# Two more pairs of gate blocks in seven-product form, and the retention norm moved to GpSimd and ScalarE one chunk later

## The chip, the cores and the metric

The kernel runs on one core of a Trainium2 chip. The metric is device time in microseconds (us), the median of several runs; smaller is better. The engines are TensorE (PE, with its weight loads shown as PEld), VectorE (DVE), ScalarE (ACT), GpSimd (POOL) and SyncE (SP, which only issues transfers here). Each works through its own instructions in program order; they wait for one another through semaphores.

## The reference

One decoder block on 1024 tokens of width 1024, in float32: two parallel token mixers (chunkwise retention and dilated attention), gated and merged, then an MLP. What matters here is the retention branch and its gate.

```python
proj = h @ w_in
rq, rk, rv, rg = parts[0], parts[1], parts[2], parts[3]   # 4 heads: dk 256, dv 512
...
def step(state, inp):                                     # a chunk of 128 tokens, 8 chunks
    s = einsum('bhid,bhjd->bhij', qi, ki) * inner_decay
    o = einsum('bhij,bhje->bhie', s, vi) + einsum('bhid,bhde->bhie', qi, state) * q_decay
    state = state * chunk_decay + einsum('bhjd,bhje->bhde', ki * k_decay, vi)
...
ro = (ro - mu) * rsqrt(var + GN_EPS)                      # mean and variance over dv
ro = ro * gn_g + gn_b
ret_out = (silu(rg) * ro) @ w_ret_out
```

## The kernel before, in words

All products are done in float32 accuracy by three passes (`mm3`, L203): each operand is split into a high and a low part, and low x high, high x low and high x high are summed, so that a product of 128x128 weights with 512 columns takes three matmuls (L207, L209, L211). The order of the work on each engine is the order in which the program writes it (a manual schedule).

The stages around the change, in time: the values of one attention group, then the **pair stage** (`queries_keys`, L1259): the projections whose results are kept in DRAM are done as pairs of two blocks of 128 output columns by `Blocks` (L226), in a Strassen-Winograd form with seven block products (`ORDER`) where eight would be needed; a pair is 7 x 4 x 3 = 84 matmuls. `PAIRS` (L1158) lists 22 pairs by kind: r (queries and keys of retention), a and k (attention), g (gates) and s (the fourth of each head's four 128-column blocks of the retention gate rg, two heads to a pair). Then the **values stage** (`values`, L1384). In both, `mod_turn` (L1243) loads one 512 KB row block of the modulation weights at a fixed number of product steps and multiplies it on DVE.

Then the **chunk loop** (`chunk`, L715), 32 chunks: heads h = 0 to 3, c = 0 to 7, g = 8h + c. In one chunk TensorE does, in this order:

- kv: the new part of the state from k and v of this chunk, two halves of three matmuls (not in c = 7)
- `rg_mm`: steps of the projection of the other three gate blocks of each head (classical: a block has eight steps of six matmuls, two halves of 512 tokens), all but the last step of this chunk; the number of steps of each chunk stands in `RG` (L693), three nearly everywhere
- `s_kt(g + 1)` (L630): the scores sT of the next chunk and the transposed keys kT; ACT and DVE then make sm, smh, sml and kh, kl from them
- o: the output of this chunk, six matmuls with the state (not in c = 0) and three with v
- `on_T` (L670): oT, the transposes of the chunk before's normalized output `on`, copied by ACT to a tile per head
- the last `rg_mm` step of the chunk

On the other engines: DVE updates the state (L745), ACT casts it to its high part (L749) and DVE subtracts for the low part (L750). `jit_qk` makes the high and low parts j of a later chunk's queries and keys (ACT L616, POOL L617). DVE takes the statistics of o (`bn_stats`, `bn_aggr`, L772 to L774), POOL raises the variance to the power -1/2 (L775), DVE multiplies by the decay (L776) and normalizes o from PSUM to SBUF (`onm`, L778). A finished gate block gets its Silu on ACT (`rg_out`, L705). In chunks c = 0 to 3 of a later head, `u_final` (L681) scales and shifts a quarter of the last head's output on ACT (L688), multiplies it by the gate on DVE (L690) and stores it. `ahead(2)` splits the next gate weights (`split_w`, L197 on ACT and L198 on DVE).

Space in PSUM (eight banks): "mm" has two buffers of two banks (the gate blocks take one each in turn), "s" has four single banks for everything else, o among it. In SBUF the tag "E" has twelve tiles of 128x1024, for the normalized output of two heads and for the gates.

Of the kernel before, what the change touches and what calls it, by code (L numbers as in the profile page):

```python
# [11 lines left out]
F32 = mybir.dt.float32  # L12
# [9 lines left out]
H = 4  # L22
# [15 lines left out]

CS_ID = 0
CS_KDEC = 128  # L40
CS_QD = 132
CS_QD2 = 136
CS_ONE = 140
CS_MH = 141
CS_W = 149
# [95 lines left out]
def block_kernel(ctx, tc, io, stop=None, dbg=None):  # L141
# [3 lines left out]
    def fv(t):  # L145
        return t.bitcast(F32)
# [18 lines left out]

    def ps_mm(name):
        return PS["p"].tile([P, 2, 512], F32, tag="mm", bufs=2, name=name)

    def ps_s(name, shape=(P, 512)):
        return PS["p"].tile(list(shape), F32, tag="s", bufs=PS["n"], name=name)  # L170
# [339 lines left out]
        R["p"] = ret_ctx.enter_context(tc.tile_pool(name="ret", bufs=1, reuse_waits="tile"))  # L510

    def etile(name, dt=F32):
        return R["p"].tile([P, 1024], dt, tag="E", bufs=12, name=name)

# [112 lines left out]
            R[n] = p.tile([P, 2, P], F32R, tag=n, bufs=1, name=n + "00")  # L627
        R["j"] = p.tile([P, 2, 4, C], F32R, tag="j", bufs=2, name="j2")

    def s_kt(i):  # L630

        p = R["p"]
        g = i
        h, c = divmod(g, NC)
        t = hd["j", g]
        ps = ps_s(f"sT{h}{c}")
        for i in range(2):
            nc.tensor.matmul(ps[:, :2 * C], t[:, 0, 2 + i, :], t[:, :, i, :], start=i == 0, stop=False,
                             skip_group_check=True)
            nc.tensor.matmul(ps[:, :C], t[:, 1, 2 + i, :], t[:, 0, i, :], start=False, stop=i == 1,  # L640
                             skip_group_check=True)
# [10 lines left out]
        nc.scalar.copy(sm, ps[:, :C])  # L652
# [12 lines left out]
        if pk is not None:  # L665
            nc.vector.scalar_tensor_tensor(flat(kl), flat(pk), kd, fv(flat(kh)), op0=ALU.mult, op1=ALU.subtract)
            hd["k", g] = (kh, kl)
        nc.vector.tensor_sub(sml, sm, fv(smh))

    def on_T(h, c):  # L670

        po = ps_s(f"oT{h}{c}", (P, 4, P))
        on = hd["o", h, c]
        if c == 0:
            hd["on", h] = [etile(f"on{h}{e}") for e in range(4)]
        for e in range(4):
            nc.tensor.transpose(po[:, e, :], on[:, e * P:(e + 1) * P], ident)
        for e in range(4):
            nc.scalar.copy(hd["on", h][e][:, c * C:(c + 1) * C], po[:, e, :])

    def u_final(h, es=range(4), queue=nc.sync):  # L681
        for e in es:
            i = h * 4 + e
            t = hd["on", h][e]
            for hf in range(2):
                neg = 16 if hf == i % 2 else 0
                b = t[:, 512 * hf:512 * hf + 512]
                nc.scalar.activation(b, b, AF.Identity, scale=gnv[0][:, neg + i:neg + i + 1],  # L688
                                     bias=gnv[1][:, neg + i:neg + i + 1])
            nc.vector.tensor_mul(t, t, hd["srg", h, e])  # L690
            queue.dma_start(y_d[h][:, 2 * (i % 2):2 * (i % 2) + 2, e // 2], t.rearrange("p (t x) -> p t x", t=2))
# [12 lines left out]

    def rg_out(h, c):  # L705

        if "rgs" in hd:
            e = {1: 0, 2: 0, 4: 1, 5: 1, 7: 2}[c]
            hd["srg", h, e] = etile(f"srg{h}{e}")
            nc.scalar.activation(hd["srg", h, e], flat(hd.pop("rgs")), AF.Silu)  # L710
        if c == 6:
            hd["srg", h, 3] = etile(f"srg{h}3")
            nc.sync.dma_start(hd["srg", h, 3], srg_d[h])

    def chunk(h, c, ahead, w=None):  # L715
        p = R["p"]
# [17 lines left out]
                kvs.append(kv)  # L734
        if g == 0:
            s_kt(1)
        rg_mm(1 if g == 0 else RG[h][c] - 1)
        for i, kv in enumerate(kvs):
            if g == 0:
                nc.scalar.copy(sh1[:, i, :], kv)  # L740
# [3 lines left out]
            else:  # L744
                nc.vector.scalar_tensor_tensor(st[:, i, :], st[:, i, :], float(GAMMA[h] ** C), kv,  # L745
                                               op0=ALU.mult, op1=ALU.add)
        if g > 0:
            for i in range(len(kvs)):
                nc.scalar.copy(sh1[:, i, :], st[:, i, :])  # L749
                nc.vector.tensor_sub(sl1[:, i, :], st[:, i, :], fv(sh1[:, i, :]))  # L750
        if g == 0:
            jit_qk(2)
        ahead(2)
        if 0 < g < NG - 1:
            s_kt(g + 1)
        po = ps_s(f"o{h}{c}")
        if c > 0:
            t = hd["j", g]
            for i in range(2):
# [5 lines left out]
            jit_qk(g + 2)  # L765
        if g > 0:
            on_T(*divmod(g - 1, NC))
        rg_mm(0 if g == 0 else 1)
        bn = p.tile([P, 6], F32, tag="bn", bufs=2, name=f"bn{h}{c}")
        ba = p.tile([P, 2], F32, tag="ba", bufs=2, name=f"ba{h}{c}")  # L770
        gr = p.tile([P, 1], F32, tag="gr", bufs=2, name=f"gr{h}{c}")
        nc.vector.bn_stats(bn, po)  # L772
        nc.vector.bn_aggr(ba, bn)
        nc.vector.tensor_scalar(gr, ba[:, 1:2], ct[:, CS_QD2 + h:CS_QD2 + h + 1], GN_EPS, op0=ALU.mult, op1=ALU.add)  # L774
# [6 lines left out]
        if h > 0 and c < 4:  # L781
            u_final(h - 1, (c,))

    def wsplit(ap):
        return ap, split_w
# [5 lines left out]
    srg_d = [dram.tile([P, S], F32, name=f"srgd{h}") for h in range(H)]  # L791
    h12_d = [dram.tile([P, 2, 512], F32, name=f"h12d{m}") for m in range(4)]
    xn, wa = [], []

# [330 lines left out]
    def sums_of_h(name, ms=range(4)):  # L1125

        for m in ms:
# [18 lines left out]
            if name != "t4":  # L1146
# [42 lines left out]
    def a_out(q, n, x, y=None):  # L1189
# [19 lines left out]
        if n in ("12", "21"):  # L1209
# [4 lines left out]
            elif pair[0] == "k":  # L1214
                dst = ak_d[pair[2], i]
            elif pair[0] == "s":
                dst = srg_d[2 * pair[1] + i]
            else:
                return
            nc.sync.dma_start(dst, OA[q][i])  # L1220
# [210 lines left out]
    steps.add(more_values, manual=True)  # L1431
    steps.add(queries_keys, manual=True)

    for h in range(H):
        for c in range(NC):
            steps.add((lambda h, c: lambda ahead, *w: chunk(h, c, ahead, *w))(h, c),
                      ([wsplit(io["w_rg"][3 * h + (0, 2, 5).index(c)])] if c in (0, 2, 5) else []),
                      manual=True)


# [390 lines left out]
    def att_step(pair, a):  # L1831

        def body(*args):
            ps = ps_mm(f"ak{pair}1{a}")
            gen = with_sums(proj_gen(ps, args[-1]))
            if a == 1:
# [991 lines left out]
def _constants():  # L2828
# [9 lines left out]
    for h in range(H):  # L2838
# [4 lines left out]
        cst[:, CS_QD + h] = np.exp(lg * (i + 1))  # L2843
        cst[:, CS_QD2 + h] = np.exp(2 * lg * (i + 1))
    cst[:, CS_ONE] = 1.0
    cst[:, CS_MH:CS_MH + 8] = -0.5

# [16 lines left out]
def pack(x, c, w_ada, b_ada, norm1_g, w_in, rel_bias, ret_gn_g, ret_gn_b,  # L2864
# [17 lines left out]
        "w_rg": _cols(w[:, 4096:6144].reshape(1024, 4, 4, P)[:, :, :3].reshape(1024, 1536)),  # L2882
        "w_rg2": _pairs(w[:, 4096:6144].reshape(1024, 4, 4, P)[:, :, 3].reshape(1024, 512)),
# [33 lines left out]
```

## Time and profile before

| | before |
|---|---|
| median of 3 runs | 2175.04 us (2174.86 to 2175.66) |
| the profiled execution | 2173.28 us, span 2171.3 us |
| mean granted TensorE clock | 0.999 |
| busy: PE, DVE, ACT, POOL | 99%, 70%, 44%, 8% of the span |
| pair stage, first to last matmul start | 179.7 to 595.7 us |
| chunk loop | about 712 to 981 us |

In the rows below, a line of the timeline has the start in us, the duration, the engine, the line of the kernel, the operation, out<-in, the shape and how many were merged into it; in brackets stands the engine's idle time before it and what ended that. A group's row has the count, the busy time in us and the mean ns of one, and then the idle time before. A row of waits has the waiting engine and its output, what it waited for, the total in us, how often, and the longest.

### The profile page before, as it was taken

Reading aid. Unit: us, or ns where it says so; the run is one execution under the profiler, and the core shown is the slowest. Engines: PE = TensorE matmul, PEld = TensorE weight load, DVE = VectorE, ACT = ScalarE, POOL = GpSimd, SP = SyncE. Lnnn points to the kernel's source line nnn. Section 1 sums busy time; section 2 is a strip of 40 time slices with the busy share of each in tenths; the row PEclk is TensorE's granted clock in tenths of the full one; section 3 lists DMA queues with packets and bytes.
Section 4 is the critical chain, followed back from the end, with each engine's and each line's share of the span. In section 5 each row is a group of like instructions: output and inputs, shape, how many; then the busy total and the mean of one; then the engine's idle time right before and its main releaser. Section 6 shows DMA issues by size and latency. Waiting matters only on the chain. (4 is left out here: it accounts for less than half of the span.)

```text
span 2171.3 us, 27289 instructions
## 1 busy us (share of the span) xinstructions
PE 2144.7 (99%) x10036; PEld 1782.4 (82%) x10036; DVE 1520.4 (70%) x2358; ACT 959.3 (44%) x1757; POOL 165.7 (8%) x199
## 2 busy tenths in 40 slices
PE   8999999999999999999999999999999999999998
PEld 6888888888887788888888888888778888888887
DVE  6886777777656677776667644677876665877855
ACT  5543322323334455556656625434454455533413
POOL 0001111100001112211110000001000000000003
PEclk9999999999999999999999999999999999999999
DMA  9859998835588744436877366653144435645322
GB/s 383 282 208 309 285 306 265 243 117 194 186 301 303 234 148 151 160 127 197 218 194 196 115 245 211 217 191 132 64 175 160 150 136 193 253 135 173 109 88 78
DMA packets 162674, 425.18 MB, mean 196 GB/s; under 512 B 28005, under 2 KB 55916, under 8 KB 159468
## 3 DMA queue, kind: packets, MB, share of 16 engines
q1 hardware_dynamic: 150264, 374.90, 48.3%
q0 software_dynamic: 9584, 48.24, 9.9%
q8 instruction: 79, 1.29, 0.2%
q10 hardware_dynamic: 2692, 0.30, 0.1%
q14 instruction: 55, 0.45, 0.1%
HBM read 324.13 MB, written 160.32 MB: 223 GB/s over the span
## 5 line engine op out<-in xcount | busy, mean ns | idle before, releaser
L207 PE MATMUL qap<-hh,qaw 128*128 128x512 f32 x264 | 102.7, 389 | 0.0
L209 PE MATMUL qap<-hl,qaw 128*128 128x512 f32 x264 | 102.7, 389 | 0.0
L211 PE MATMUL qap<-hh,qaw 128*128 128x512 f32 x264 | 102.7, 389 | 0.0
L617 POOL TENSOR_TENSOR j<-qk,j 128x512 fp32r<-128x512 f32 x32 | 42.8, 1338 | 454.8 <-ACT j L616 454.8
L2235 POOL TENSOR_TENSOR accnf<-accnf,sqnf 128x256 f32<-128x256 f32 (+1 forms) x18 | 16.6, 922 | 609.6 <-ACT sqnf L2231 609.6
L2339 ACT ACTIVATE a<-a 128x512 f32<-128x512 f32 x48 | 30.3, 631 | 72.8 <-DVE a L2338 71.3
L749 ACT CAST stateh<-state 128x512 fp32r<-128x512 f32 x54 | 32.9, 622 | 57.8 <-DVE state L745 55.7
L209 PEld LDWEIGHTS qap<-hl,qaw 128*128 128x128 f32 x264 | 49.5, 188 | 10.4
L211 PEld LDWEIGHTS qap<-hh,qaw 128*128 128x128 f32 x264 | 49.6, 188 | 10.3
L207 PEld LDWEIGHTS qap<-hh,qaw 128*128 128x128 f32 x264 | 49.5, 188 | 10.2
L2547 ACT CAST w2h<-w2s 128x512 fp32r<-128x512 f32 x36 | 22.4, 621 | 80.3 <-DVE w2s L2585 80.3
L264 DVE TENSOR_TENSOR fw<-w1r,fw 128x512 fp32r<-128x512 f32 x48 | 32.9, 688 | 33.6 <-ACT fw L254 33.6
L264 DVE TENSOR_TENSOR qaw<-wa,qaw 128x512 fp32r<-128x512 f32 x66 | 44.0, 687 | 9.4 <-ACT qaw L254 9.4
L2070 DVE TENSOR_TENSOR rwl<-rwl,rwh 128x1024 fp32r<-128x1024 f32 x25 | 30.2, 1221 | 29.0 <-ACT rwh L2100 29.0
L207 PE MATMUL fp<-h2h,fw 128*128 128x512 f32 x128 | 50.0, 390 | 0.0
L209 PE MATMUL fp<-h2l,fw 128*128 128x512 f32 x128 | 49.8, 389 | 0.0
L211 PE MATMUL fp<-h2h,fw 128*128 128x512 f32 x128 | 49.8, 389 | 0.0
L207 PE MATMUL roa<-rh,rwl 128*128 128x512 f32 x128 | 49.8, 389 | 0.0
L209 PE MATMUL roa<-rl,rwh 128*128 128x512 f32 x128 | 49.8, 389 | 0.0
L211 PE MATMUL roa<-rh,rwh 128*128 128x512 f32 x128 | 49.8, 389 | 0.0
L1603 ACT ACTIVATE P<-P,ng 128x128 f32<-128x128 f32 (+1 forms) x96 | 41.9, 438 | 17.6 <-DVE ng L1595 17.5
L292 DVE TENSOR_TENSOR qat<-qat,qap 128x512 f32<-128x512 f32 x22 | 15.1, 688 | 42.8 <-PE qap L211 35.8
(3089 smaller groups left out, 7187.8 us busy)
## 6 DMA issues: line engine op xcount, KB each, us to landing
cossin<-in_w_ada_dram SPq DMA_DIRECT2D x32, 512.0 KB, 3.5
v<-vd SPq DMA_DIRECT2D x32, 512.0 KB, 4.3
w1r<-in_w_ff_dram SPq DMA_DIRECT2D x32, 512.0 KB, 4.6
yt<-y POOLq DMA_DIRECT2D x24, 512.0 KB, 7.5
xsd<-as SPq DMA_DIRECT2D x24, 512.0 KB, 3.1
w2r<-in_w_ff2s_dram SPq DMA_DIRECT2D x24, 512.0 KB, 6.4
em<-in_w_ada_dram SPq DMA_DIRECT2D x16, 512.0 KB, 10.2
wrvs<-in_w_rv_dram POOLq DMA_DIRECT2D x16, 512.0 KB, 9.8
```

Source lines behind the costliest of these rows:

```text
L207: nc.tensor.matmul(o, wl, xh, start=first, stop=False, skip_group_check=skip)
L209: nc.tensor.matmul(o, wh, xl, start=False, stop=False, skip_group_check=skip)
L211: nc.tensor.matmul(o, wh, xh, start=False, stop=last, skip_group_check=skip)
L264: nc.vector.tensor_sub(t[:, 512:], src, fv(t[:, :512]))
L292: nc.vector.tensor_sub(u, u, b)
L617: nc.gpsimd.tensor_sub(t[:, 1], src, fv(t[:, 0]))
L749: nc.scalar.copy(sh1[:, i, :], st[:, i, :])
L1603: nc.scalar.activation(v, v, AF.Exp, bias=ng[:, blk:blk + 1], accum_out=st[:, g, blk, 2 + a:3 + a])
L2070: nc.vector.tensor_sub(lo, fv(lo), fv(hi))
L2235: (nc.vector if f == 7 else nc.gpsimd).tensor_add(G["acc", key], G["acc", key], sq)
L2339: nc.scalar.activation(o, o, AF.Relu)
L2547: nc.scalar.copy(hi, src)
```

## The change

- The third and the fourth gate block of each head are now one s pair: four s pairs where there were two (`PAIRS` ends in "agagassss", 24 pairs), and eight blocks are left to the chunk loop where there were twelve. Two gates per head are loaded back from DRAM, in c = 4 and c = 6.
- `RG` falls to 64 steps in all. Weights are requested one chunk ahead of the chunk in which their block begins.
- A gate block takes two single banks of a new tag "rg" with two buffers, and its two Silus follow its last product at once. o gets a tag of its own, "o", with two buffers. At the first attention step PSUM is laid out anew (`banks(False)`).
- The normalization of chunk g is one ACT activation with scale and bias, issued in chunk g + 1 behind `s_kt` and ahead of o. The decay is folded into the epsilon (`CS_EQ`), so no multiplication by the decay is left; POOL makes scale and bias in three operations of 128x1.
- The two low halves of the state are apart: one inside `s_kt`, the other behind the statistics of o. `ahead(2)` moves behind the statistics. The multiplication and store of `u_final` come one chunk later.
- `on_T` copies two blocks at once into a double tile (tag "EO", four buffers); "E" has four buffers, for gates alone.
- `mod_turn` issues a load every two steps, where before it was every 16/7.

```diff
+    def ps_rg(name):
+        return PS["p"].tile([P, 512], F32, tag="rg", bufs=2, name=name)
+    def ps_o(name):
+        return PS["p"].tile([P, 512], F32, tag="o", bufs=2, name=name)
...
     def etile(name, dt=F32):
-        return R["p"].tile([P, 1024], dt, tag="E", bufs=12, name=name)
+        return R["p"].tile([P, 1024], dt, tag="E", bufs=4, name=name)
...
-    def s_kt(i):
+    def s_kt(i, mid=None):
...
             hd["k", g] = (kh, kl)
+        if mid:
+            mid()
         nc.vector.tensor_sub(sml, sm, fv(smh))
...
-        for e in range(4):
-            nc.scalar.copy(hd["on", h][e][:, c * C:(c + 1) * C], po[:, e, :])
+        for e in range(2):
+            nc.scalar.copy(hd["on2", h][e][:, :, c * C:(c + 1) * C], po[:, 2 * e:2 * e + 2, :])
...
-    RG = ((6, 2, 2, 3, 3, 3, 3, 2),) + ((3,) * NC,) * (H - 1)
+    RG = (6, 2, 2, 2, 1, 1, 2, 3), (3, 2, 2, 2, 1, 1, 2, 3), (3, 2, 2, 2, 1, 1, 2, 3), (3, 2, 2, 2, 1, 1, 1, 1)
...
-                hd["rgk"], hd["rgw"], hd["rgp"] = 0, hd["rgws"].pop(0), ps_mm("rg")
+                hd["rgk"], hd["rgw"], hd["rgp"] = 0, hd["rgws"].pop(0), [ps_rg(f"rg{i}") for i in range(2)]
             proj_mm(hd["rgp"], hd["rgw"], [hd["rgk"]])
             hd["rgk"] += 1
             if hd["rgk"] == NK:
-                hd["rgs"] = hd["rgp"]
+                i = hd["rgi"] = hd.get("rgi", -1) + 1
+                t = hd["srg", i // 2, i % 2] = etile(f"srg{i // 2}{i % 2}")
+                for j, ps in enumerate(hd["rgp"]):
+                    nc.scalar.activation(t[:, 512 * j:512 * j + 512], ps, AF.Silu)
...
-        rg_mm(1 if g == 0 else RG[h][c] - 1)
+        rg_mm(1 if g == 0 else RG[h][c] - (g < NG - 1))
...
-        if g > 0:
-            for i in range(len(kvs)):
+        def low(i):
+            nc.vector.tensor_sub(sl1[:, i, :], st[:, i, :], fv(sh1[:, i, :]))
+        if g > 0 and kvs:
+            for i in range(2):
                 nc.scalar.copy(sh1[:, i, :], st[:, i, :])
-                nc.vector.tensor_sub(sl1[:, i, :], st[:, i, :], fv(sh1[:, i, :]))
...
-        ahead(2)
+        if g == NG - 1:
+            ahead(2)
         if 0 < g < NG - 1:
-            s_kt(g + 1)
-        po = ps_s(f"o{h}{c}")
+            s_kt(g + 1, (lambda: low(0)) if kvs else None)
+        if "onm" in hd:
+            hd.pop("onm")()
+        po = ps_o(f"o{h}{c}")
...
         nc.vector.bn_stats(bn, po)
         nc.vector.bn_aggr(ba, bn)
-        nc.vector.tensor_scalar(gr, ba[:, 1:2], ct[:, CS_QD2 + h:CS_QD2 + h + 1], GN_EPS, op0=ALU.mult, op1=ALU.add)
-        nc.gpsimd.tensor_tensor(gr, gr, mhalf[:, 0:1], op=ALU.pow)
-        nc.vector.tensor_mul(gr, gr, ct[:, CS_QD + h:CS_QD + h + 1])
+        nc.vector.tensor_scalar_add(gr[:, 0:1], ba[:, 1:2], ct[:, CS_EQ + h:CS_EQ + h + 1])
+        nc.gpsimd.tensor_tensor(gr[:, 2:3], ba[:, 0:1], ct[:, CS_NEG:CS_NEG + 1], op=ALU.mult)
+        nc.gpsimd.tensor_tensor(gr[:, 1:2], gr[:, 0:1], mhalf[:, 0:1], op=ALU.pow)
+        nc.gpsimd.tensor_tensor(gr[:, 2:3], gr[:, 1:2], gr[:, 2:3], op=ALU.mult)
+        if g > 0 and kvs:
+            low(1)
+        if g < NG - 1:
+            ahead(2)
+        if "um" in hd:
+            hd.pop("um")()
+        if h > 0 and c < 4:
+            hd["um"] = u_final(h - 1, (c,), late=True)
         on = p.tile([P, DV], F32, tag="on", bufs=1, name=f"onm{h}{c}")
-        nc.vector.tensor_scalar(on, po, ba[:, 0:1], gr, op0=ALU.subtract, op1=ALU.mult)
+        hd["onm"] = lambda: nc.scalar.activation(on, po, AF.Identity, scale=gr[:, 1:2], bias=gr[:, 2:3])
+        if g == NG - 1:
+            hd.pop("onm")()
...
-    s_pairs = [("s", i) for i in range(H // 2)]
+    s_pairs = [("s", i) for i in range(H)]
...
-             for i in "rargrarkrargrarkgagass"]
+             for i in "rargrarkrargrarkgagassss"]
...
-        while turn["i"] < NV + 2 and 7 * turn["n"] > 16 * turn["i"]:
+        while turn["i"] < NV + 2 and turn["n"] > 2 * turn["i"]:
...
+    RGW, n = [], 0
+    for g in range(NG):
+        RGW += [g - (g > 1)] * (n < 8 * len(RGW) + 1 <= n + RG[g // NC][g % NC])
+        n += RG[g // NC][g % NC]
```

More of the change, by code (lines that the diff above doesn't have):

```diff
@@ L40 @@
 CS_KDEC = 128
-CS_QD = 132
-CS_QD2 = 136
+CS_NEG = 132
+CS_EQ = 136
 CS_ONE = 140
@@ L674, in on_T, with u_final @@
         if c == 0:
-            hd["on", h] = [etile(f"on{h}{e}") for e in range(4)]
+            hd["on2", h] = [R["p"].tile([P, 2, 1024], F32, tag="EO", bufs=4, name=f"on{h}{e}") for e in range(2)]
+            hd["on", h] = [hd["on2", h][e // 2][:, e % 2] for e in range(4)]
         for e in range(4):
             nc.tensor.transpose(po[:, e, :], on[:, e * P:(e + 1) * P], ident)
-        for e in range(4):
-            nc.scalar.copy(hd["on", h][e][:, c * C:(c + 1) * C], po[:, e, :])
-    def u_final(h, es=range(4), queue=nc.sync):
+        for e in range(2):
+            nc.scalar.copy(hd["on2", h][e][:, :, c * C:(c + 1) * C], po[:, 2 * e:2 * e + 2, :])
+    def u_final(h, es=range(4), queue=nc.sync, late=False):
         for e in es:
@@ L689, in u_final, with mul @@
                                      bias=gnv[1][:, neg + i:neg + i + 1])
-            nc.vector.tensor_mul(t, t, hd["srg", h, e])
-            queue.dma_start(y_d[h][:, 2 * (i % 2):2 * (i % 2) + 2, e // 2], t.rearrange("p (t x) -> p t x", t=2))
-    RG = ((6, 2, 2, 3, 3, 3, 3, 2),) + ((3,) * NC,) * (H - 1)
+            def mul(t=t, i=i, e=e):
+                nc.vector.tensor_mul(t, t, hd["srg", h, e])
+                queue.dma_start(y_d[h][:, 2 * (i % 2):2 * (i % 2) + 2, e // 2], t.rearrange("p (t x) -> p t x", t=2))
+            if late:
+                return mul
+            mul()
+    RG = (6, 2, 2, 2, 1, 1, 2, 3), (3, 2, 2, 2, 1, 1, 2, 3), (3, 2, 2, 2, 1, 1, 2, 3), (3, 2, 2, 2, 1, 1, 1, 1)
     def rg_mm(n):
@@ L767, in chunk @@
             on_T(*divmod(g - 1, NC))
[L768 removed]
+        rg_mm(1 if 0 < g < NG - 1 else 0)
         bn = p.tile([P, 6], F32, tag="bn", bufs=2, name=f"bn{h}{c}")
         ba = p.tile([P, 2], F32, tag="ba", bufs=2, name=f"ba{h}{c}")
[L771 removed]
+        gr = p.tile([P, 3], F32, tag="gr", bufs=2, name=f"gr{h}{c}")
         nc.vector.bn_stats(bn, po)
         nc.vector.bn_aggr(ba, bn)
[L774 to L776 removed]
+        nc.vector.tensor_scalar_add(gr[:, 0:1], ba[:, 1:2], ct[:, CS_EQ + h:CS_EQ + h + 1])
[10 more added lines that the diff above has]
+            hd["um"] = u_final(h - 1, (c,), late=True)
         on = p.tile([P, DV], F32, tag="on", bufs=1, name=f"onm{h}{c}")
[L778 removed]
+        hd["onm"] = lambda: nc.scalar.activation(on, po, AF.Identity, scale=gr[:, 1:2], bias=gr[:, 2:3])
+        if g == NG - 1:
+            hd.pop("onm")()
         hd["o", h, c] = on
         rg_out(h, c)
[L781 to L782 removed]
     def wsplit(ap):
@@ L790, in block_kernel @@
     ak_d = {(p, a): dram.tile([P, S], F32, name=f"akd{p}{a}") for p in range(2) for a in range(2)}
-    srg_d = [dram.tile([P, S], F32, name=f"srgd{h}") for h in range(H)]
+    srg_d = {(h, i): dram.tile([P, S], F32, name=f"srgd{h}{i}") for h in range(H) for i in range(2)}
     h12_d = [dram.tile([P, 2, 512], F32, name=f"h12d{m}") for m in range(4)]
@@ L1216, in a_out @@
             elif pair[0] == "s":
-                dst = srg_d[2 * pair[1] + i]
+                dst = srg_d[pair[1], i]
             else:
@@ L1833, in body @@
         def body(*args):
+            if pair == a == 0:
+                banks(False)
             ps = ps_mm(f"ak{pair}1{a}")
```

19 lines of the change are left out of this document (8 added, 11 removed).

## The prediction

> **What bounds the kernel now.** I read the page's busy shares first, then the busy time by stretches (the first column is the stretch, then busy time and instruction count of PE, PEld, DVE, ACT and POOL, the granted clock, the DMA share), then TensorE's list of waits.
>
> ```profile
> span 2171.3 us, 27289 instructions
> PE 2144.7 (99%) x10036; PEld 1782.4 (82%) x10036; DVE 1520.4 (70%) x2358; ACT 959.3 (44%) x1757; POOL 165.7 (8%) x199
> ...
> 560.00:598.00 38.00, 38.00 (x170) 31.45 (x169) 24.29 (x37) 11.34 (x18) 0.00 (x0) 1.00 0.50 179
> 650.00:660.00 10.00, 8.08 (x35) 6.03 (x34) 7.89 (x12) 3.78 (x6) 0.00 (x0) 1.00 0.88 357
> 733.00:982.00 249.00, 248.46 (x1229) 206.76 (x1229) 187.53 (x396) 134.11 (x337) 53.24 (x60) 1.00 0.44 145
> ...
> PE vc L209 <- DVE vwl L1328: 1.9, 2, 1.5
> PE rg L207 <- DVE vr L1367: 1.1, 1, 1.1
> ACT vo L1362 <- DMA vd<-vo: 10.6, 3, 4.7
> ...
> PE kv L207 <- DVE kl L666: 0.2, 1, 0.2
> PE o L207 <- DVE state L745: 0.2, 1, 0.2
> ```
>
> TensorE is busy in 99% of the span. The chunk loop is the stretch 733 to 982: TensorE works 248.46 of 249 us there, while DVE works 187.5 (75%), ACT 134 (54%) and POOL 53 (21%). The end of the product pairs (560 to 598) has no gap at all. So the set end is the number of matmuls, and whatever makes TensorE wait. The only gaps near the change are 1.9 us in the values stage (650 to 660, where ACT waited for the landing of a store) and 1.1 us at the first gate product; inside the chunk loop the whole list is two waits of 0.2. A busy matmul row says little about its pace, because matmuls overlap; the pace is read from start to start:
>
> ```profile
> L207 PE MATMUL qap<-hh,qaw x264: 389/389/389, 179.7 to 595.2; 128*128 128x512 f32 x132
> L211 PE MATMUL qap<-hh,qaw x264: 389/389/389, 180.2 to 595.7; 128*128 128x512 f32 x132
> ...
> 825.28 0.62 PE L207 MATMUL rg<-hh,raw_5684l 128*128 128x512 f32 x2
> 828.00 0.28 PE L638 MATMUL sT<-j 128*128 128x256 f32 x1
> ```
>
> The pair stage starts its first matmul at 179.7 and its last at 595.7, and 22 pairs of 84 are 1848 matmuls: 416.0/1847 = 0.2252 us each. In the chunk loop two rg_mm steps (twelve matmuls) take 828.00 - 825.28 = 2.72 us, 0.2267 each.
>
> **The matmuls.** Four gate blocks leave the chunk loop: 4 x 48 = 192 matmuls x 0.2267 = 43.5 us less. Two pairs of 84 come: 168 x 0.2252 = 37.8 us more. Net -5.7 us, and this is all that the change can win in matmuls. In the pair stage the new preparation, Silu and stores lie beside TensorE as they do in the stretch 560 to 598 (DVE 24.3 and ACT 11.3 of 38 us): nothing. The modulation loads now end at turn 67 of 92, where before they ended at 76 of 78, so the values stage has less traffic when its gap occurs. I take half of that 1.9 us back, -1.0; its bounds are 0 and -3.0 (both gaps).
>
> **What the cover was worth.** The gate products are also the work behind which each chunk hides its chain. Per head the rg_mm steps fall from three a chunk to (3,2,2,2,1,1,2,3), and head 3 ends in 1,1. One of them comes after the transposes oT, so between the products kv and the products sT there are r - 1: none where r is 1. And oT(g-1) now waits for the normalization onm(g-1), which ACT does inside the same chunk, behind sm, kh and smh of s_kt. First that chain where ACT and DVE are free, in a normal chunk, then the places of oT in a c = 0 chunk (only three o products) and in c = 6 (no kT):
>
> ```profile
> 777.22 0.28 PE L638 MATMUL sT<-j 128*128 128x256 f32 x1
> 777.82 0.27 ACT L652 COPY sm<-sT 128x128 f32<-128x128 f32 x1 [1.45 <-PE sT L640]
> 779.07 0.62 ACT L616 CAST j<-qk 128x512 fp32r<-128x512 f32 x1
> 779.95 0.60 PE L677 MATMUL oT<-ct,onm 128*128 128x128 f32 x4
> ...
> 852.41 0.28 PE L638 MATMUL sT<-j 128*128 128x256 f32 x1
> 853.07 0.27 ACT L652 COPY sm<-sT 128x128 f32<-128x128 f32 x1 [1.62 <-PE sT L640]
> 853.75 0.60 PE L677 MATMUL oT<-ct,onm 128*128 128x128 f32 x4
> 854.22 0.61 ACT L616 CAST j<-qk 128x512 fp32r<-128x512 f32 x1
> ...
> 836.65 0.28 PE L638 MATMUL sT<-j 128*128 128x256 f32 x1
> 839.21 0.60 PE L677 MATMUL oT<-ct,onm 128*128 128x128 f32 x4
> ...
> L749 ACT CAST stateh<-state 128x512 fp32r<-128x512 f32 x50 | 30.5, 622 | 53.1 <-DVE state L745 51.1 <-DVE state L743 2.0
> L688 ACT ACTIVATE on<-on,gnt 128x512 f32<-128x512 f32 x24 | 18.6, 838 | 0.0
> ```
>
> Counted from sT, the ACT copy sm starts at 0.60 to 0.66 and the cast j, whose place onm takes, at 1.81 to 1.85. onm has no row: it is 128x512 from PSUM with scale and bias from tiles. Its bounds are 0.62 (the plain cast L749) and 0.84 (L688, which has both operands); I take 0.80, close to L688, the nearer kind (two of them take 1.54). So it ends at 1.83 + 0.80 = 2.63, and with 0.05 to TensorE oT may start at 2.68. TensorE gets there at 2.73 in a normal chunk (free, by 0.05), at 1.34 in c = 0 and at 2.56 in c = 6. **c = 0** of heads 1 to 3: 3 x 1.34 = 4.0 us. **c = 6** of heads 0 to 2: 3 x 0.12 = 0.4.
>
> **Chunks with r = 1.** Here sT follows kv at once, and the two state casts stand ahead of sm on ACT:
>
> ```profile
> 832.56 0.39 PE L207 MATMUL kv<-v,kl 128*128 128x512 f32 x1
> 833.70 0.39 PE L211 MATMUL kv<-v,kh 128*128 128x512 f32 x1
> 833.80 1.28 DVE L745 SCALAR_TENSOR_TENSOR state<-state,kv 128x512 f32<-128x512 f32 x2
> 833.93 0.61 PE L207 MATMUL rg<-hh,raw_5955l 128*128 128x512 f32 x2
> 834.51 1.22 ACT L749 CAST stateh<-state 128x512 fp32r<-128x512 f32 x2 [1.43 <-DVE state L745]
> ...
> 817.04 1.22 DVE L690 TENSOR_TENSOR on<-on,srg 128x1024 f32<-128x1024 f32 x1
> 818.17 1.28 DVE L745 SCALAR_TENSOR_TENSOR state<-state,kv 128x512 f32<-128x512 f32 x2
> ...
> 830.93 0.70 DVE L772 BATCH_NORM_STATS2 bn<-o 128x6 f32<-128x512 f32 x1 [0.51 <-PE o L211]
> 831.89 0.21 DVE L774 TENSOR_SCALAR gr<-ba,ct 128x1 f32<-128x1 f32 x1
> 835.16 1.29 DVE L750 TENSOR_TENSOR statel<-state,stateh 128x512 fp32r<-128x512 f32 x2
> ```
>
> With T0 the start of kv (832.56): kv's second half ends at 1.53 (833.70 + 0.39), the state's second half can start at 1.56, its cast 0.71 later (833.80 to 834.51) at 2.27, and sm at 2.80 (0.62 on, less 0.1 of overlap). A free sm would start at 1.37 + 0.62 = 1.99. That is 0.81 late, less the slack of 0.05: 0.76 of waiting. In c = 4 of heads 1 to 3 the moved multiplication of u_final (L690) stands ahead on DVE: statistics at T0 - 1.63, their last step 0.96 later and 0.21 long, one half of the low state (0.65, less overlap), so it starts at 0.14 and the state at 1.27; sm comes at 3.14, waiting 1.10. In c = 5 that chunk's wait has already absorbed it. So c = 4: 0.76 + 3 x 1.10 = 4.1; c = 5: 4 x 0.76 = 3.0; c = 6 of head 3 (no kT): 0.9. Together 8.0 us. With r = 2 sT comes 1.36 later, and 0.81 or 1.15 is covered.
>
> **The gate's banks.** Before, a block had one of two double banks; now each block takes both banks of "rg", so the next block's first matmuls wait for both Silus.
>
> ```profile
> 781.32 0.62 PE L211 MATMUL rg<-hh,raw_5359h 128*128 128x512 f32 x2
> 781.98 1.03 ACT L710 ACTIVATE srg<-rg 128x1024 f32<-128x1024 f32 x1 [0.62 <-PE rg L211]
> 788.83 1.54 ACT L688 ACTIVATE on<-on,gnt 128x512 f32<-128x512 f32 x2
> ```
>
> Blocks end in the second rg_mm of chunks 1, 6, 9, 14, 17, 22, 25. After 6, 14 and 22 no kv follows (c = 7). From the row: the first half ends at 781.71, the second at 781.94, and a Silu of 512 starts 0.04 behind its half; at 0.62 each (as L749) they run to 782.37 and 782.89, so the second matmul of the next block, due at 782.01, starts at 782.93: 3 x 0.92 = 2.8 us. After chunk 1 kv covers it. After chunks 9, 17 and 25 something else is late: "E" now has four buffers, all holding the last head's gates, and the new block's tile is free only when u_final's multiplication for c = 0 has run, which is issued later in that same chunk. It ends at T0 + 1.36, the Silus at 2.02 and 2.54; the next block's second matmul, due at 1.60, starts at 2.58 (0.98 lost). u_final's two activations (1.54) follow, then the state casts to 5.10, sm at 5.00 where 4.33 was free: 0.62 more. 3 x 1.60 = 4.8 us; if the slot doesn't matter, the Silus and the two activations alone make sm 0.3 late, each time.
>
> The Trainium skill's Perfetto Trace Analysis, section Matmuls, has a rule against this edit: independent matmul groups should rotate through different PSUM banks, so that one's evacuation overlaps the next one's matmuls. By that rule alone each of the seven boundaries would pay two Silus of 0.62, 8.7 us, where I have 2.8 and 4.8; that no TensorE wait for a Silu stands in the trace of before, with its rotating banks, agrees.
>
> **Edits that I cost at nothing.** Splits of gate weights (L197, L198) move behind the statistics in c = 5 and c = 0, whose own waits hide them; without these they would be worth about 0.3 each. Two copies of 256 columns for four of 128; POOL's two more small operations per chunk (behind the j subtraction, due only a chunk later); one more gate load per head on SP's queue and u_final's store a chunk later, both ahead of needs many us away. The waiting oT holds up rg_mm and kv behind it, and thereby the next state; ACT and DVE then have the next chunk's time back, which is why waits don't add up from chunk to chunk. The two slots for o remove a reuse that costs nothing visible before. DVE loses 0.97 us a chunk, off the path.
>
> **The sum.** 4.0 + 0.4 + 8.0 + 2.8 + 4.8 = 20.0 us of waits, -5.7, -1.0: +13.3. The profiled execution took 2173.28 us (span 2171.3), 1.76 below the median of 2175.04, so 2186.6 on its own scale, 2188.3 on the median's.
>
> **Rivals.**
> - *Hidden after all, faster.* In a normal chunk the chain fits by 0.05, and ACT is 46% idle. If ACT reached onm before TensorE reached oT everywhere, 2175.04 - 6.7 = 2168.3 remains. It decides below 2.4 us of waits in all; c = 0 alone, where three products stand for nine, speaks for 4.0. Chance 0.07.
> - *A draw.* Slot and banks cost nothing and onm takes 0.62: c = 0 gives 3.5, r = 1 gives 6.4, less 6.7: 2178.2. Chance 0.08.
> - *The chain late in every chunk.* The 0.05 is thin: were the chain 0.25 longer (DVE behind its statistics), 28 chunks lose 7 us more: 2195. Chance 0.13.
> - *The clock.* If waits made the throttle cut TensorE's clock, a chunk of 8.65 us (828.00 to 836.65) at half pace costs up to 8.65; once in three heads, 26 us: 2214. The stretch 650 to 660 kept 1.00 through 1.9 us of gap, and my longest wait is shorter. Chance 0.02. The Trainium skill's TensorE: Matmul & The Clock Gate, section HAM oscillation, says the clock falls when TensorE idles over about 3.4 us; by that rule it stays at 1.00 here, with which the row agrees.
>
> The forecast itself has 0.70.
>
> **How the numbers follow.** Low end: onm at 0.62 takes 2.5 us off, no slot wait 3.9, both old gaps gone 2.0: +4.9, near 2180. High end: the late chain, 2195, and a little of the statistics' spread: 2196. A measurement of this kernel can tell about 0.2% (4.4 us) from no change. Faster 0.07, same 0.08, slower 0.70 + 0.13 + 0.02 = 0.85.
>
> **What would show it.** Right: TensorE waits at oT for ACT's onm, about 1.3 us in c = 0 and 0.8 to 1.1 in c = 4 and 5; rg waiting for srg's Silu behind chunks 6, 14, 22 and, with DVE's L690 equivalent ahead of the Silu, behind 9, 17, 25; the pair stage longer by 37.8 us. Wrong: a chunk loop without TensorE waits, oT waits under 0.3 us, or new gaps before 712 or behind 982, where I expect none.

## The result, and the profile after

The changed kernel takes 2189.22 us (median of 5 runs, 2187.53 to 2191.26) against 2174.99 us before (5 runs, 2173.95 to 2175.66). The ratio is 1.0067, 95% interval 1.0054 to 1.0081: slower by 14.2 us. Its profiled execution took 2191.26 us, 2.0 above its median, while that of before was 1.7 below its own, so the two traces differ by more (spans 2189.5 and 2171.3, +18.2) than the medians do.

The page's busy shares, then the list of TensorE's waits (total us, times, longest), then two stretches (length, busy time and count of PE, PEld, DVE, ACT and POOL, granted clock, DMA): the one that was shown of before, and the chunk loop of after:

```profile
span 2189.5 us, 27376 instructions
PE 2147.1 (98%) x10012; PEld 1778.4 (81%) x10012; DVE 1513.0 (69%) x2322; ACT 983.8 (45%) x1749; POOL 205.3 (9%) x263
...
PE oT L686 <- ACT onm L807: 14.2, 14, 2.0
PE pb L447 <- DMA onehot<-in_onehot_dram: 6.0, 2, 3.7
PE rg L213 <- ACT srg L721: 4.0, 6, 1.0
...
PE va L213 <- ACT va L1405: 1.0, 1, 1.0
...
733.00:982.00 249.00, 232.74 (x1133) 186.95 (x1133) 169.08 (x340) 146.97 (x309) 97.75 (x126) 0.99 0.56 185
749.10:997.90 248.80, 230.21 (x1126) 183.98 (x1125) 169.11 (x350) 150.93 (x320) 95.07 (x123) 0.99 0.51 165
```

TensorE runs 24 matmuls less (10012 for 10036), as counted. Two lines are new and head the list: oT waiting for ACT's onm (14 times, 14.2 us) and the gate products waiting for ACT's Silu (6 times, 4.0 us). In the same 249 us TensorE is now busy for 232.74 where it was for 248.46, although DVE fell from 187.5 to 169.1 and ACT is busy for only 147 of the 249. That stretch begins 16 us ahead of after's chunk loop; the loop itself, in the last row, shows the same. So neither engine became the bound: TensorE waits for a chain that is late.

The bracket of a TensorE row counts from the modelled end of the last matmul. From start to start the loss is larger, and these rows show by how much:

```profile
820.45 0.40 PE L217 MATMUL o<-v,smh 128*128 128x512 f32 x1
821.98 0.66 PE L686 MATMUL oT<-ct,onm 128*128 128x128 f32 x4 [1.13 <-ACT onm L807]
...
806.50 0.61 PE L217 MATMUL rg<-hh,raw_5632h 128*128 128x512 f32 x2
807.58 0.99 PE L213 MATMUL rg<-hh,raw_5634l 128*128 128x512 f32 x2 [0.46 <-ACT srg L721]
808.41 0.62 PE L215 MATMUL rg<-hl,raw_5634h 128*128 128x512 f32 x2
...
832.29 0.39 PE L217 MATMUL kv<-v,kh 128*128 128x512 f32 x1
833.68 0.99 PE L213 MATMUL rg<-hh,raw_5717l 128*128 128x512 f32 x2 [1.01 <-ACT srg L721]
834.51 0.63 PE L215 MATMUL rg<-hl,raw_5717h 128*128 128x512 f32 x2
```

At 0.23 a matmul oT was due at 820.68 and started at 821.98: 1.30, bracket plus 0.17. The new gate block's third matmul was due at 806.50 + 4 x 0.2267 = 807.41 and came at 808.41: 1.00, since its second matmul waits for a Silu of its own. Behind the c = 0 chunk it was due at 832.97 and came at 834.51: 1.54.

By stages, from matmul starts. The row `qap<-hh,qaw`, whose last start the table before the change gives as the end of the pair stage, is not its last: twelve more matmuls of another weight tile follow, to 598.4 us before and 638.2 us after. The differences are the same with either end; the table keeps the first.

| stage, us | before | after | difference | predicted |
|---|---|---|---|---|
| pair stage (first to last start of `qap<-hh,qaw`) | 416.0 | 454.1 | +38.1 | +37.8 |
| values (from there to the first rg) | 116.7 | 113.6 | -3.1 | -1.0 |
| chunk loop (first rg to the next stage's first ak) | 268.3 | 248.7 | -19.6 | -43.5 + 20.0 = -23.5 |
| before the pairs and behind the loop | 1370.3 | 1373.1 | +2.8 | 0 |

### The profile page after: what moved, and what is told of

Read it like the earlier page. It is cut to its first block, busy times and chain, and to the rows that moved or that the text cites. A ratio compares the mean times of both kernels' runs of the same rounds, so it can differ in the third digit from the quotient of the medians.

```text
span 2189.5 us, 27376 instructions
## 1 busy us (share of the span) xinstructions
PE 2147.1 (98%) x10012; PEld 1778.4 (81%) x10012; DVE 1513.0 (69%) x2322; ACT 983.8 (45%) x1749; POOL 205.3 (9%) x263
## 5 line engine op out<-in xcount | busy, mean ns | idle before, releaser
L213 PE MATMUL qap<-hh,qaw 128*128 128x512 f32 x288 | 112.0, 389 | 0.0
L215 PE MATMUL qap<-hl,qaw 128*128 128x512 f32 x288 | 112.0, 389 | 0.0
L217 PE MATMUL qap<-hh,qaw 128*128 128x512 f32 x288 | 112.0, 389 | 0.0
L213 PEld LDWEIGHTS qap<-hh,qaw 128*128 128x128 f32 x288 | 54.1, 188 | 11.2
L217 PEld LDWEIGHTS qap<-hh,qaw 128*128 128x128 f32 x288 | 54.1, 188 | 11.2
L215 PEld LDWEIGHTS qap<-hl,qaw 128*128 128x128 f32 x288 | 54.1, 188 | 11.2
L659 DVE TENSOR_TENSOR sm<-sm,sT 128x128 f32<-128x128 f32 x32 | 9.2, 288 | 53.9 <-ACT sm L658 53.9
```

The costliest lines, as they stand in the source:

```text
L213: nc.tensor.matmul(o, wl, xh, start=first, stop=False, skip_group_check=skip)
L215: nc.tensor.matmul(o, wh, xl, start=False, stop=False, skip_group_check=skip)
L217: nc.tensor.matmul(o, wh, xh, start=False, stop=last, skip_group_check=skip)
```

## The experiments

All start from the changed kernel. The chunk-loop time is that of the table, from each run's own trace.

**The gate tile: load_late.** The prediction said that behind chunks 9, 17 and 25 the Silu finds no free tile of "E". Here the fourth gate of a head is loaded a head later, in c = 2.

```diff
-        if c in (4, 6):
-            e = c // 2
-            hd["srg", h, e] = etile(f"srg{h}{e}")
-            nc.sync.dma_start(hd["srg", h, e], srg_d[h, e - 2])
+        for hh_, e in {4: [(h, 2)], 2: [(h - 1, 3)] if h else [], 6: [(h, 3)] if h == H - 1 else []}.get(c, []):
+            hd["srg", hh_, e] = etile(f"srg{hh_}{e}")
+            nc.sync.dma_start(hd["srg", hh_, e], srg_d[hh_, e - 2])
```

> The fourth gate of a head is loaded in c = 2 of the next head (head 3: still c = 6), so that a free E tile waits for the block that ends in c = 1. Theory (waits for tiles and for the norm cost the time): the waits of rg for srg behind chunks 9, 17 and 25 go, with what they delay, 3 x 1.3 us: about 2185. Rival (the slot is not what holds the Silu): 2189, rows of rg waiting for srg unchanged at six.

Measured: 2184.62 us, ratio 1.0046 (1.0030 to 1.0063), 4.6 us less. The interval overlaps that of the change (1.0054 to 1.0081), but each of its four runs (2182.25 to 2185.73) is faster than each of the change's five. Its two wait lines:

```profile
PE oT L686 <- ACT onm L806: 14.3, 14, 2.0
...
PE rg L213 <- ACT srg L721: 1.4, 3, 0.5
```

The three tile waits are gone; the three bank waits (0.46 each) and all oT waits stay. The tile was the cause of the first kind alone, as said.

**The transposes later: oT_late.** The gate step that stands behind oT is put ahead of it, as cover for the chain.

```diff
-        if g > 0:
-            on_T(*divmod(g - 1, NC))
         rg_mm(1 if 0 < g < NG - 1 else 0)
+        if g > 0:
+            on_T(*divmod(g - 1, NC))
```

> The transposes oT are issued behind the chunk's last gate step, 1.36 us later on TensorE; nothing else. Theory (TensorE waits for the norm on ACT inside the chunk): nearly all waits of oT for onm go, some 12 to 15 us: 2174 to 2177. Rival (the gate's banks and tiles cost most, or a lower clock does): 3 us at most, 2186 or more, and the wait moves to the next kv.

Measured: 2183.4 us, ratio 1.0038 (1.0023 to 1.0053): a gain of 5.8, less than half of what was expected. The oT waits did fall, from 14.2 to 4.7. But:

```profile
PE rg L213 <- ACT srg L721: 7.6, 6, 2.2
...
PE oT L686 <- ACT onm L807: 4.7, 6, 1.0
...
827.52 1.08 ACT L721 ACTIVATE srg<-rg 128x512 f32<-128x512 f32 x2 [3.14 <-DVE on L701]
...
828.16 1.28 PE L213 MATMUL rg<-hh,raw_5717l 128*128 128x512 f32 x2 [2.16 <-ACT srg L721]
829.24 1.06 PE L215 MATMUL rg<-hl,raw_5717h 128*128 128x512 f32 x2
830.10 1.05 PE L217 MATMUL rg<-hh,raw_5717h 128*128 128x512 f32 x2
```

The gate block now ends earlier, and its Silu stands still for 3.14 us until DVE's L701 frees the tile; TensorE waits 2.16 there instead of 1.01. Behind that wait the matmuls run at half pace (two in 1.05 instead of 0.62), and so they do behind a second one of 2.18: the clock, below.

**Both: oT_late_load.** The two edits together.

> Both edits: oT behind the last gate step, and the fourth gate loaded in the next head. In oT_late the three largest waits left (2.2 us, rg for srg behind chunks 9, 17 and 25) were due to the E slot, and behind two of them the clock fell in the trace. Theory: these three and the two stretches of low clock go, about 6.6 + 3.4 us off 2183.4: 2173 to 2175, clock at 1.00 all through the chunk loop. Rival (waits only move on): rg waits for srg of the same sum elsewhere, 2180 or more.

Measured: 2174.65 us, ratio 0.9999 (0.9990 to 1.0008): no difference from before. Chunk loop 233.8, clock 1.00 throughout. 4.6 and 5.8 alone make 10.4; together they give 14.6. The Silu waits that oT_late had made longer are gone (1.0 us in all for 7.6), and with them its two stretches of low clock, some 1.5 us each; 7.1 us of oT waits are left in eight places.

**The cover spread evenly: flat.** `RG` gives two steps to every chunk, so no chunk has r = 1 but the last four, and the blocks end in c = 1 and c = 5 (the last in c = 7), with the next chunk's kv behind them.

```diff
-    RG = (6, 2, 2, 2, 1, 1, 2, 3), (3, 2, 2, 2, 1, 1, 2, 3), (3, 2, 2, 2, 1, 1, 2, 3), (3, 2, 2, 2, 1, 1, 1, 1)
+    RG = (6, 2, 2, 2, 2, 2, 2, 2), (2,) * NC, (2,) * NC, (2, 2, 2, 2, 1, 1, 1, 1)
```

> The gate steps are two in every chunk (head 3 ends 1,1,1,1), so heads 0 to 2 have no chunk with r = 1 and no block ends ahead of c = 7. Theory: the waits in c = 4 and 5 of heads 0 to 2 go (about 5 us) and those of rg behind chunks 6, 14, 22 (about 3), c = 0 stays: 2181 to 2183. Rival (cover as a whole is too small, the steps only move it): 2189, as many waits in other chunks.

Measured: 2180.94 us, ratio 1.0029 (1.0018 to 1.0040), 8.3 less: oT 10.6 in 10 waits for 14.2 in 14, rg 2.7 in 3 for 4.0 in 6. The bank waits are gone, since the three left are those for the tile. Of the six oT waits in c = 4 and 5 of heads 0 to 2 four are gone, where all six had been expected to go; 0.89 each is left in c = 5 of heads 1 and 2. That the time came out as expected is in part the clock: after's stretch of low clock, some 1.5 us, is not in flat's trace.

**The norm earlier: norm_now.** ACT's onm is issued at the end of its own chunk.

```diff
-        if g == NG - 1:
-            hd.pop("onm")()
+        hd.pop("onm")()
```

> The norm's activation is issued at the end of its own chunk on ACT, behind POOL's three operations, not in the next chunk. Theory (oT waits because the norm stands behind sm, kh and smh): no wait of oT for onm is left, ACT waits about 2 us a chunk for POOL ahead of the state casts, which r of 2 or more covers: 2174 to 2178. Rival (the deferral is needed, since ACT held by POOL delays casts and sm): waits of o, kv or sT of 0.5 us and more in most chunks, 2189 or slower.

Measured: 2186.03 us, ratio 1.0050 (1.0035 to 1.0065): a miss. The oT waits are gone (0.2 us in all), but the list is headed by the other line:

```profile
PE rg L213 <- ACT srg L721: 9.2, 6, 2.3
...
PE ak L213 <- DVE raw_7244l L204: 2.5, 1, 2.5
```

Without oT's waits the gate blocks end before their tile is free, as in oT_late: 2.32, 1.97 and 1.92 us behind chunks 9, 17 and 25. Two of the three bank waits grew as well (0.97 and 1.57 for 0.46), and behind four of these six waits the clock fell, some 1.5 us each. I had taken away one of two waits in series.

**The norm on DVE again: norm_dve_load.** As before the change, DVE normalizes o in its own chunk; the fourth gate is loaded late.

```diff
+        on = p.tile([P, DV], F32, tag="on", bufs=1, name=f"onm{h}{c}")
+        nc.vector.tensor_scalar(on, po, ba[:, 0:1], gr[:, 1:2], op0=ALU.subtract, op1=ALU.mult)
...
-        hd["onm"] = lambda: nc.scalar.activation(on, po, AF.Identity, scale=gr[:, 1:2], bias=gr[:, 2:3])
```

> As load_late, but the norm stays on DVE in its own chunk (scale from POOL's power, one DVE pass over o), as in the kernel before. Theory: no oT waits for a norm, so the 14 us of them in load_late go; r = 1 chunks keep a little: 2170 to 2174. Rival (with shorter chunks DVE becomes the bound, so the norm had to move): kv or sT waiting for DVE, 0.5 us or more in most chunks, 2180 or more.

Measured: 2190.56 us, ratio 1.0072 (1.0058 to 1.0086): a miss. The rival's time came true, its sign only in part.

```profile
PE rg L213 <- ACT srg L721: 6.1, 3, 2.0
...
PE kv L213 <- DVE kl L672: 3.9, 10, 0.4
PE oT L686 <- DVE state L759: 3.3, 6, 0.6
...
PE sT L644 <- POOL j L623: 2.0, 7, 0.3
```

DVE's own results (kl, state) are now waited for 16 times, but by 0.3 to 0.6 us, 7.2 in all, not by 0.5 or more in most chunks. The largest line is another: three Silu waits of 2.0 behind chunks 6, 14 and 22, each with a stretch of low clock behind it (some 1.5 us). There the state update stands on DVE behind the norm and a weight split, and ACT's casts, sm and the Silus wait for it. So the norm on DVE lengthens the chain; that DVE has no room for it isn't shown, since DVE is busy for 184.5 of the loop's 251.3 us, and no run tried the norm on DVE with the even steps of flat, which take these three boundaries away.

**Chunk 1: split_early.** The longest wait, 1.96 us, is oT of chunk 0 in chunk 1. In after's trace a weight split stands ahead of the state update on DVE, and the matmuls behind the wait run at half pace:

```profile
763.36 1.22 DVE L204 TENSOR_TENSOR raw_5632l<-raw,raw_5632h 128x1024 fp32r<-128x1024 f32 x1 [0.63 <-ACT raw_5632h L203]
...
764.50 1.28 DVE L760 SCALAR_TENSOR_TENSOR state<-state,kv 128x512 f32<-128x512 f32 x2
...
765.21 1.22 ACT L767 CAST stateh<-state 128x512 fp32r<-128x512 f32 x2 [1.94 <-DVE state L760]
...
766.33 0.26 ACT L658 COPY sm<-sT 128x128 f32<-128x128 f32 x1
...
767.48 0.77 ACT L807 ACTIVATE onm<-o,gr 128x512 f32<-128x512 f32 x1
...
768.30 1.04 PE L686 MATMUL oT<-ct,onm 128*128 128x128 f32 x4 [1.96 <-ACT onm L807]
...
770.00 1.05 PE L215 MATMUL rg<-hl,raw_5630h 128*128 128x512 f32 x2
...
766.10:769.50 3.40, 1.44 (x7) 1.18 (x6) 2.77 (x9) 2.47 (x7) 0.67 (x1) 0.84 0.99 315
769.50:772.90 3.40, 3.40 (x11) 2.66 (x10) 1.39 (x3) 1.62 (x4) 1.91 (x4) 0.66 0.99 322
```

The split of chunk 0 goes back ahead of the statistics:

```diff
-        if g == NG - 1:
+        if g in (0, NG - 1):
             ahead(2)
...
-        if g < NG - 1:
+        if 0 < g < NG - 1:
             ahead(2)
```

> The changed kernel with one move: in chunk 0 alone the split of the two gate weights (ahead(2)) runs in its old place, ahead of the output statistics, so that it is not ahead of chunk 1's state update on DVE. Theory: the late weight split is what makes chunk 1's oT wait 1.96 us, and that wait is what halves the clock behind it; the wait falls to about 0.9 and the clock stays at 1.00 there, 1.07 + 1.7 = 2.8 us less, about 2186.4, and nothing else moves. Rival: the chain of chunk 1 is late for its own length (state, casts, sm, onm), the split only sits in it; then the wait stays at 1.8 to 2.0 and the time at 2189.

Measured: 2187.51 us, ratio 1.0055 (1.0041 to 1.0069); its interval overlaps that of the change (1.0054 to 1.0081), so no gain is shown. The wait grew instead:

```profile
759.54 1.42 DVE L204 TENSOR_TENSOR raw_5632l<-raw,raw_5632h 128x1024 fp32r<-128x1024 f32 x1 [0.73 <-issue]
760.89 0.68 DVE L792 BATCH_NORM_STATS2 bn<-o 128x6 f32<-128x512 f32 x1
...
761.95 1.27 DVE L760 SCALAR_TENSOR_TENSOR state<-state,kv 128x512 f32<-128x512 f32 x2
...
765.76 0.65 PE L686 MATMUL oT<-ct,onm 128*128 128x128 f32 x4 [2.25 <-ACT onm L807]
...
763.50:766.90 3.40, 1.15 (x8) 1.06 (x8) 2.71 (x9) 2.86 (x8) 0.61 (x1) 1.00 1.04 361
```

My theory fell: wherever the split stands in chunk 0, it and the statistics are both ahead of chunk 1's state on DVE, so the order between them buys nothing. Whether the wait goes when the split stands behind that state update was not run. And the clock stayed at 1.00 behind a longer wait, so the wait's length alone does not lower it.

**The values stage: mod_old.** The old pace and start of the modulation loads.

```diff
-    MOD0 = 16 * len(ORDER) + 4
+    MOD0 = 18 * len(ORDER) + 4
...
-        while turn["i"] < NV + 2 and turn["n"] > 2 * turn["i"]:
+        while turn["i"] < NV + 2 and 7 * turn["n"] > 16 * turn["i"]:
```

> The modulation loads have their old pace and start two pairs later, so that they end as near to the chunk loop as before. Read from the stages of its trace: if the earlier end of these loads is what shortened the values stage (113.6 us after, 116.7 before), it comes back to 116 to 117; if the two new pairs or the shifted start did it, it stays at 113 to 114. Chunk loop unchanged at 247 to 249.

Measured: one run of 2193.16 us. The values stage stays at 113.6, that of after. So the faster loads are not what shortened it, though I had argued so in the prediction. The chunk loop took 251.0, not 247 to 249: kv of chunk 1 waits 1.26 us for the landing of v, which it does in no other trace, and the oT wait behind it is 2.54 instead of 1.96, with a stretch of low clock. One execution can't tell whether the older pace of the loads is the cause.

**Towards a better version.** oT_load_flat_split joins oT_late, load_late, flat and split_early:

> oT behind the last gate step, the fourth gate loaded in the next head, two gate steps in every chunk, and the first chunk's weight split in its old place. Theory: in heads 0 to 2 no wait over 0.6 us is left, head 3 keeps two or three from r = 1: the product saving (5.7) and the values stage (3) come through nearly whole: 2167 to 2169, faster than before. Rival (the chunk loop can't run with two gate steps a chunk): not faster than before, 2174 or more.

Measured: 2168.37 us, ratio 0.9971 (0.9960 to 0.9983), faster than both kernels. Chunk loop 228.3; six oT waits of 0.5 to 1.0 are left, 5.2 in all. Three of them, of 0.9, are in heads 0 to 2, where none over 0.6 had been expected. norm_now_load_flat removes these by joining norm_now, load_late and flat:

> The changed kernel with three edits: onm is issued at the end of its own chunk on ScalarE, the fourth gate tile of a head is loaded one head later, and RG is two steps a chunk (head 3 2,2,2,2,1,1,1,1). Theory: norm_now's Silu waits were the free tile and the uneven blocks; without them oT finds onm ready and the gate products wait for Silus by under 0.5 us each, 2167 to 2171, like the version with oT behind the gate products. Rival: onm at the end of a chunk stands on ScalarE ahead of the Silus whatever tile is free; waits of 1.5 to 2.3 for the Silu remain with clock drops behind some, 2174 to 2182.

Measured: 2168.09 us, ratio 0.9966 (0.9954 to 0.9978), as the theory had it. No wait for a Silu is left, so norm_now's were the tile and the uneven blocks, in shares that this run doesn't tell apart. One long wait stands at the loop's end, 2.51 us of ak for the split of its weights, whose cast stands behind the last onm and Silu on ACT. In norm_now_load_flat_end that split is issued ahead of the last chunk's gate products:

```diff
+        if g == NG - 1:
+            ahead(2)
         rg_mm(1 if g == 0 else RG[h][c] - (g < NG - 1))
...
-        if g == NG - 1:
-            ahead(2)
```

> The kernel norm_now_load_flat (onm in its own chunk, the fourth gate loaded a head later, RG two a chunk) with one more move: in the last chunk the split of the next stage's weights (ahead(2)) is issued ahead of the gate products instead of ahead of o. Theory: its one long TensorE wait, 2.51 us of ak for the low half of that split, arises because the cast of the split stands behind the last onm and the last Silu on ScalarE; issued earlier both are done in time and about 2.3 us go, 2165 to 2167. Rival: the split's weights land late or its place delays sm and o of the last chunk by as much, 2168.

Measured: 2166.2 us, ratio 0.9950 (0.9936 to 0.9963). TensorE over its chunk loop, and what is left of the waits:

```profile
747.60:972.00 224.40, 222.30 (x1125) 184.71 (x1124) 159.98 (x350) 148.33 (x322) 92.74 (x123) 1.00 0.56 183
...
961.48 0.39 PE L644 MATMUL sT<-j 128*128 128x256 f32 x1 [0.29 <-POOL j L623]
...
972.00 0.70 PE L213 MATMUL ak<-hh,raw_7242l 128*128 128x512 f32 x2 [1.63 <-DVE raw_7242l L204]
```

The loop takes 224.4 us: 268.3 - 43.5 = 224.8 is what the removed matmuls alone would leave. The ak wait fell by 0.9 only, not by the 2.3 expected: on ACT the split's cast (969.56) now stands behind the onm of chunk 30 (968.89), which itself waits 2.45 us for POOL. Behind this wait, too, the clock fell. Against norm_now_load_flat the step is 1.9 us, with overlapping intervals; against before it is a gain of 10 us.

## Why the prediction was right, point by point

The sign, the size (+13.3 forecast, +14.2 measured) and the mechanism stood. But the sum hides errors of both signs, and the two traces, from which every term below is read, differ by +18.2: that the forecast comes within 1 us of the medians is in part luck.

- **Matmuls.** -43.5 and +37.8: the pair stage measured +38.1. The pace of 0.2252 had the wrong end: 1848 matmuls start from 179.7 to 598.4, so the pace is 0.2267 as in the chunk loop, 168 matmuls take 38.1 us, and the net is -5.4 instead of -5.7. And the best version's loop, with about as much waiting left (1.9 us) as before's had, confirms the -43.5 to within 0.4.
- **c = 0.** Predicted 3 x 1.34; the three brackets are 1.13, with 0.17 each 3 x 1.30 = 3.9. onm takes 0.77 us (0.80 assumed).
- **c = 6 with r = 2.** Predicted 0.4; no wait is seen there.
- **r = 1.** Predicted 8.0, measured 9.9. These are head 0's two, the first of each kind of the other heads, and c = 6 of head 3:

```profile
791.13 0.66 PE L686 MATMUL oT<-ct,onm 128*128 128x128 f32 x4 [0.53 <-ACT onm L807]
797.81 0.66 PE L686 MATMUL oT<-ct,onm 128*128 128x128 f32 x4 [0.53 <-ACT onm L807]
...
852.92 0.66 PE L686 MATMUL oT<-ct,onm 128*128 128x128 f32 x4 [1.05 <-ACT onm L807]
860.16 0.66 PE L686 MATMUL oT<-ct,onm 128*128 128x128 f32 x4 [1.09 <-ACT onm L807]
...
991.32 0.66 PE L686 MATMUL oT<-ct,onm 128*128 128x128 f32 x4 [0.70 <-ACT onm L807]
```

  In c = 4 and 5 of head 0 the loss is 0.70 each (0.76 predicted), in c = 6 of head 3 it is 0.87 (0.9), in c = 4 of the other heads 1.20 to 1.38 (1.10). The step that failed is "In c = 5 that chunk's wait has already absorbed it": there the loss is 1.26 to 1.28 each, not 0.76.
- **Banks.** 3 x 0.92 predicted, 3 x 1.00 measured. The Trainium skill's rule on rotating banks (Perfetto Trace Analysis, section Matmuls) points the right way, but the 8.7 us that I worked out from it for seven boundaries is not what is seen: three boundaries pay 1.00. Where kv stands between, nothing is paid: not behind chunk 1, and not behind chunks 9, 17 and 25 once the tile is free (load_late).
- **The free tile.** 3 x 1.60 predicted; 1.54, 1.35 and 1.35 measured, 4.2 in all, and load_late takes 4.6 back. The split inside was wrong: 0.98 at the gate and 0.62 in the next chunk's chain were forecast, but all of it lies at the gate, and oT of c = 1 does not wait.
- **Chunk 1, not priced.** I counted the splits that moved at nothing and had no term for g = 1, where oT's chain starts behind head 0's first state. It waits 2.1 us. Of what lies behind, oT to kv take 771.70 - 768.30 = 3.40 us where load_late, at full clock, takes 1.88: 1.5 more in this execution.
- **Chunk 31, not priced.** A bracket of 0.53 at its oT: 0.70.
- **Before's own waits.** These stood in the old chunk loop (before's list of waits) and are gone, with 0.17 each 1.8 us. The prediction read only the two of 0.2 from the list, overlooked the 0.9, and credited none:

```profile
PE kv L207 <- ACT state L763: 0.9, 1, 0.9
...
PE kv L207 <- DVE kl L666: 0.2, 1, 0.2
...
PE o L207 <- DVE state L745: 0.2, 1, 0.2
```

- **The values stage.** -3.1 for -1.0. Both old gaps (1.9 and 1.1) went, the far bound that I had named, and another of 1.0 came. mod_old refutes my reason; the cause is open.

The loop adds up: -43.5 - 1.8 + (3.9 + 9.9 + 3.0 + 4.2 + 2.1 + 1.5 + 0.7) = -20.0, measured -19.6. The 2.8 us outside the stages (1.7 of it ahead of the pairs, where the wait for the one-hot load differs by 1.0) belong to no step of mine; in the eleven experiments' traces the first qap starts between 179.9 and 181.1, so most of it is the spread between executions.

Of the rivals, "the chain late in every chunk" did not come: the slack of 0.05 held in every chunk with r = 2 but chunk 1. The rival that the clock falls had the chance 0.02 for a wrong reason: the 1.9 us that kept the clock at 1.00 were two gaps, of 0.46 and 1.46, and my longest wait, 1.96, is longer than both. It came true in a small form, once and for 1.5 us instead of a chunk at half pace.

## What to carry to other kernels

Work that is taken off the critical engine takes its cover with it: before removing products, list every chain that ran behind them and price each place where the cover becomes shorter, first and last iterations included. Waits in series hide one another: removing the first showed the second in two experiments (oT_late, norm_now), and the joint edits paid most, so pair an earlier consumer with the buffer that it will then need. Spread the remaining cover evenly before moving any operation: one line of the table of steps gave 8.3 us, some 1.5 of them from the clock.

## What was not expected of the hardware

Behind some TensorE waits of 1.6 to 2.5 us the granted clock fell for one stretch of 3.4 us, at a loss of some 1.5 us, and behind others of the same length it did not. The two 3.4 us windows about such a place read 0.84 and 0.66, as above: together half of one window's clock is missing. The traces show what most of the difference comes from. In the traces each such stretch is 3.413 us long at 0.50, and the changes of the clock lie whole multiples of 3.413 us apart: in norm_now 238, 17, 10, 7 and 357 such windows lie before, between and behind its four low ones. Cutting each trace on this fixed grid gives, for the window that holds most of the wait:

| run | wait, us | window from | TensorE idle in it, us | clock in the next window |
|---|---|---|---|---|
| mod_old | 2.54 | 766.85 | 2.53 | 0.50 |
| norm_now | 2.32 | 824.48 | 2.32 | 0.50 |
| oT_late | 2.16 | 825.10 | 2.16 | 0.50 |
| oT_late | 2.18 | 886.54 | 2.11 | 0.50 |
| norm_dve_load (three) | 2.03 to 2.04 | 800.51, 865.37, 930.22 | 2.03 to 2.04 | 0.50 |
| norm_now | 1.97 | 885.92 | 1.97 | 0.50 |
| after | 1.96 | 765.01 | 1.96 | 0.50 |
| split_early | 2.25 | 761.96 | 1.87 | 1.00 |
| norm_now | 1.92 | 950.77 | 1.85 | 0.50 |
| oT_late | 2.20 | 947.98 | 1.76 | 1.00 |
| norm_now_load_flat | 2.51 | 973.52 | 1.73 | 1.00 |
| flat | 1.96 | 764.17 | 1.71 | 1.00 |
| norm_now_load_flat_end | 1.63 | 969.47 | 1.69 | 0.50 |
| load_late | 1.96 | 762.47 | 1.59 | 1.00 |
| norm_now | 1.57 | 923.46 | 1.57 | 0.50 |
| before | 1.46 | 656.26 | 1.46 | 1.00 |

All nine windows with 1.96 us of idle time or more were followed by one at half clock, and none with 1.46 or less was; no window that isn't in the table has as much. The same wait of 1.96 in the same place lies whole in one window in after, and is shared by two in load_late and flat, where the clock stayed at 1.00. So where a wait falls on the grid counts, not its length alone. One kernel may thus lose these 1.5 us in one execution and not in the next; that isn't shown, since one execution of each was traced. Between 1.57 and 1.87 both are seen (three of eight fell), and what decides there is open; the idle times are counted from modelled ends of matmuls. The Trainium skill's TensorE: Matmul & The Clock Gate, section HAM oscillation, names idle times over about 3.4 us; here shorter ones were enough.
